# Two branch projections of a hybrid S5 and RG-LRU layer: seven products on halves in place of eight

## The chip, the cores and the metric
One core of a Trainium2 chip. The metric is the time of one execution on the device in microseconds, median of three runs; 1832.1 us before the change (1831.18 to 1832.52). Five engines work beside each other: TensorE (PE) multiplies into PSUM, VectorE (DVE), ScalarE (ACT) and GpSimd (POOL) work element by element, and SyncE (SP) issues the transfers between memory and SBUF, one behind the other in the order of its queue.

## What is computed
One layer for 512 prompt tokens and 8 x 4 sample tokens, 544 in all, in float32. After a norm, one input projection gives the inputs of two branches. Branch A (1024 channels) runs an S5 scan and a GLU, branch B (2048 channels) a convolution and a gated recurrence. The part that the change touches is the merge:

```
y = y * jax.nn.sigmoid(y @ p["s5_w_glu"] + p["s5_b_glu"])          # end of branch A, 1024 x 1024
...
y_a = y_a * jax.nn.silu(z_a)
y_b = y_b * jax.nn.silu(z_b)
merged = (jax.nn.sigmoid(g_a) * (y_a @ p["w_proj_a"])              # 1024 x 2048
          + jax.nn.sigmoid(g_b) * (y_b @ p["w_proj_b"]))           # 2048 x 2048
out = merged @ p["w_out"]                                          # 2048 x 2048
x = x + gate[:, None] * out
```

## The kernel before
Channels lie on the partitions in blocks of 128, tokens in the columns. To keep float32 accuracy, each weight and each input is split into a high and a low part (float32r): ScalarE copies the value into the high part, VectorE subtracts the high part from the value to get the low one. For 1024 weight columns a partition that is lines 144 and 145 (`split_w`), for an input block of 544 tokens lines 179 and 181 (`split_x`). One product of two blocks is then three matmuls, high x high, high x low and low x high. `product` (lines 165 to 174, matmul on line 172) does this for one block of output channels, over all blocks of input channels and both halves of the tokens (272 columns, one PSUM bank each).

Weights come by SyncE in pieces of 1 MB (`weights`, `raw`, three buffers); the high and low parts have four buffers each. Results that a later stage needs (the branch outputs `ygd` and `ybd`, the gates `zad`, `gad` and `gbd`, the gated first projection `pad`) pass through memory and come back by `loaded` into four buffers named `ld`.

The stages in question, in this order:
- GLU (lines 922 to 933): for 8 output blocks, 48 matmuls each, ScalarE takes the sigmoid, VectorE multiplies twice, and the block is split into `ah` and `al`.
- First projection (lines 936 to 948): 16 output blocks of 48 matmuls. VectorE multiplies each half with the gate from PSUM, the result goes to `pad`, and one block of the other branch's output is loaded and split into `bh`, `bl`.
- Second projection (lines 951 to 964): 16 output blocks of 96 matmuls, gated, added to what comes back from `pad`, and split for the output projection; the last eight splits follow behind the loop, when the buffers of `bh` and `bl` come free.
- Output projection (lines 974 on, matmul on line 993).

All element-wise helpers go through `tt` (line 403). The code is written in stage order; a scheduler sets the order of the instructions on each engine from its own estimate of their times, and engines keep that order. GpSimd has no work between the end of branch B and the output projection.

Of the kernel before, what the change touches and what calls it, by code (L numbers as in the profile page):

```python
# [32 lines left out]
NCH = TP // L     # chunks of the prompt  # L33
CU = 82           # columns of a group: chunks | spare | sample | sample, late
CS0 = NCH + 1     # sample sequences in the slots 0..3 (for y)
CS1 = CS0 + NS    # sample sequences in the slots 4..7 (for the last state)
WIN = 96          # columns moved in one product
CY = 74

# RG-LRU: the flat time axis, 512 prompt tokens, then 3 + 4 columns a sequence  # L40
FT = TP + NS * (TS + 3)

O_U, O_ZA, O_XB, O_ZB, O_GA, O_GB = 0, 8, 16, 32, 48, 64  # column blocks of w_in
# [12 lines left out]
def tile_hybrid_s5_rglru(  # L56
# [11 lines left out]
    dq = nc.sync      # weights  # L68
    dq2 = nc.sync   # small loads and what passes through DRAM

    const = ctx.enter_context(tc.tile_pool(name="const", bufs=1))
    wpool = ctx.enter_context(tc.tile_pool(name="wpool", bufs=4))
# [15 lines left out]
    # what passes through DRAM  # L88
# [19 lines left out]
    def exact_exp(out, x, n, e):  # L108
        """exp(x) to the last bits: 2^n times a polynomial; n and e are scratch."""
# [5 lines left out]
        # 2^n: the exponent bits of ScalarE's 2^(n + 1/4)  # L115
# [10 lines left out]
    def rsqrt_mean(eng, out, ss, u):  # L126
        """1 / sqrt(ss / D + EPS), one Newton step behind ScalarE's root; ss and u are scratch."""
# [9 lines left out]
    def split_w(src, to=None):  # L137
        """A float32 [P, 1024] as the sum of two float32r tiles."""
# [12 lines left out]
    def weights(w, col, kt, room=split_w):  # L151
        """Columns of w as stationary operands: (block, k) -> (high, low)."""
# [908 lines left out]
```

## Time and profile before

| | |
|---|---|
| median of three runs | 1832.1 us |
| profiled execution, first to last instruction | 1828.9 us |
| TensorE busy | 1755.0 us (96%), 13,420 matmuls |
| VectorE, ScalarE, GpSimd busy | 930.7 us (51%), 738.0 us (40%), 149.5 us (8%) |
| transfers | 281.58 MB, 154 GB/s on average |

The span of the profiled execution is 3.2 us shorter than the median of the timed runs, which also hold what lies around the instructions. Busy shares are averages over stages; the windows by stage in the rows below cut the span at the starts of the GLU (about 1275), of the first projection (1324), of the second (1421) and of the output projection (1616).

### The profile page before, as it was taken

The numbers are of one execution on the slowest core, as the hardware profiler recorded it, in microseconds if no ns is written. First come the engines' busy times: TensorE is split into PE (matmuls) and PEld (weight loads), VectorE is DVE, ScalarE is ACT, GpSimd is POOL, SyncE is SP. The second block draws the span as 40 slices with busy tenths as digits, with TensorE's granted clock in tenths as the row PEclk, the third lists the DMA queues.
The fourth block names the chain that finished last, engine by engine and source line by source line (L and its number), as shares of the span: only waits on it lengthen the run. The fifth ranks groups of instructions, "written<-read, shape, count | busy, mean of one in ns | idle before, by whom it ended". The sixth has DMA issues, their size and how long they took to land.

```text
span 1828.9 us, 32708 instructions
## 1 busy us (share of the span) xinstructions
PE 1755.0 (96%) x13420; PEld 1691.1 (92%) x13420; DVE 930.7 (51%) x1584; ACT 738.0 (40%) x1134; POOL 149.5 (8%) x385
## 2 busy tenths in 40 slices
PE   7879999999959999999999999999999999999997
PEld 4558999999949999999999999999999999999997
DVE  4695255547973223324556565655543433355654
ACT  7774232332212222223555545555333322234543
POOL 2100000000000000011222122321000000000000
PEclk9899999999979999999999999999999999999999
DMA  9787535444235546443444453542677644376682
GB/s 327 261 283 189 132 93 138 110 117 111 79 86 134 138 106 167 124 132 109 142 134 118 126 166 120 155 146 94 221 254 214 179 131 128 105 221 177 172 226 93
DMA packets 400280, 281.58 MB, mean 154 GB/s; under 512 B 68513, under 2 KB 350457, under 8 KB 398905
## 3 DMA queue, kind: packets, MB, share of 16 engines
q1 hardware_dynamic: 400130, 279.49, 52.5%
q8 instruction: 105, 1.72, 0.4%
q14 instruction: 45, 0.37, 0.1%
HBM read 244.64 MB, written 32.44 MB: 152 GB/s over the span
## 4 chain that ended last, share of the span: by engine, by line
PE 77%; DVE 9%; DMA 7%; ACT 3%; issue 2%; SPq 2%; POOL 0%; ACTq 0%; DVEq 0%; POOLq 0%
PE acc L172 57%; PE acc L993 11%; DVE lo L145 2%; DVE t L403 2%; DVE v L403 2%; DMA raw<-in_w_ada_dram 1%; PE pg L845 1%; PE gacc L785 1%; PE ada L218 1%; DMA raw<-in_w_in_dram 1%; DVE eh L403 1%; DMA ld<-zad 1%; PE py L652 1%; PE py L650 1%; PE pk L629 1%
## 5 line engine op out<-in xcount | busy, mean ns | idle before, releaser
L145 DVE TENSOR_TENSOR lo<-raw,hi 128x1024 fp32r<-128x1024 f32 x374 | 455.3, 1223 | 568.7 <-ACT hi L144 561.4
L172 PE MATMUL acc<-xh,hi 128*128 128x272 f32 x3424 | 719.6, 290 | 4.9 <-ACT adasb L228 2.7
L172 PE MATMUL acc<-xh,lo 128*128 128x272 f32 x3424 | 717.4, 289 | 1.3 <-DVE lo L145 1.3
L172 PE MATMUL acc<-xl,hi 128*128 128x272 f32 x3424 | 717.0, 290 | 0.2 <-DVE xl L181 0.2
L144 ACT ACTIVATE hi<-raw 128x1024 fp32r<-128x1024 f32 x374 | 391.2, 1056 | 674.9 <-PE acc L172 547.8
L172 PEld LDWEIGHTS acc<-xh,hi 128*128 128x128 f32 x3424 | 541.3, 189 | 11.0 <-ACT adasb L228 3.2
L172 PEld LDWEIGHTS acc<-xl,hi 128*128 128x128 f32 x3424 | 541.2, 189 | 1.7 <-DVE xl L181 0.5
L172 PEld LDWEIGHTS acc<-xh,lo 128*128 128x128 f32 x3424 | 539.5, 189 | 2.5 <-DVE lo L145 1.7
L993 PE MATMUL acc<-xl,hi 128*128 128x288 f32 (+1 forms) x512 | 149.3, 292 | 0.0
L993 PE MATMUL acc<-xh,hi 128*128 128x288 f32 (+1 forms) x512 | 148.6, 291 | 0.0
L993 PE MATMUL acc<-xh,lo 128*128 128x288 f32 (+1 forms) x512 | 147.3, 288 | 0.0
L993 PEld LDWEIGHTS acc<-xh,lo 128*128 128x128 f32 x512 | 96.6, 189 | 0.1
L993 PEld LDWEIGHTS acc<-xl,hi 128*128 128x128 f32 x512 | 96.5, 188 | 0.3
L993 PEld LDWEIGHTS acc<-xh,hi 128*128 128x128 f32 x512 | 96.2, 188 | 0.1
L403 DVE TENSOR_TENSOR ld<-acc,ld 128x272 f32<-128x272 f32 x64 | 25.2, 434 | 57.5 <-PE acc L172 57.5
L218 PE MATMUL ada<-lo,cs 128*72 128x512 f32 x128 | 45.3, 438 | 8.2 <-DVE lo L145 7.6
L218 PE MATMUL ada<-hi,cs 128*72 128x512 f32 x128 | 44.6, 432 | 7.4 <-ACT hi L144 7.3
L729 ACT ACTIVATE r<-pg,c 128x284 f32<-128x284 f32 x64 | 29.7, 492 | 39.7 <-PE pg L845 39.7
L650 PE MATMUL py<-eh,ca 128*128 128x96 f32 x128 | 25.7, 284 | 20.6 <-DVE eh L403 20.6
L181 DVE TENSOR_TENSOR xl<-ld,xh 128x544 fp32r<-128x544 f32 x24 | 17.3, 723 | 47.0 <-ACT xh L179 46.9
L654 ACT ACTIVATE y<-py 128x296 f32<-128x296 f32 x16 | 6.7, 419 | 85.0 <-PE py L652 66.2
L650 PEld LDWEIGHTS py<-eh,ca 128*128 128x128 f32 x128 | 20.5, 200 | 21.5 <-issue 20.8
(304 smaller groups left out, 1445.5 us busy)
## 6 DMA issues: line engine op xcount, KB each, us to landing
raw<-in_w_in_dram SPq DMA_DIRECT2D x80, 1024.0 KB
raw<-in_w_ada_dram SPq DMA_DIRECT2D x64, 512.0 KB
raw<-in_w_out_dram SPq DMA_DIRECT2D x32, 1024.0 KB
raw<-in_w_ada_dram SPq DMA_DIRECT2D x16, 1024.0 KB
raw<-in_w_proj_b_dram SPq DMA_DIRECT2D x16, 1024.0 KB
raw<-in_w_proj_a_dram SPq DMA_DIRECT2D x8, 1024.0 KB
u<-ud SPq DMA_DIRECT2D x128, 41.0 KB
gad<-sg SPq DMA_DIRECT2D x16, 272.0 KB
```

What stands on the lines that cost most here:

```text
L144: act.activation(hv, src, AF.Copy)
L145: dve.tensor_tensor(out=lv, in0=src, in1=hv, op=SUB)
L172: pe.matmul(acc[j][:, :HT], lhsT=w_, rhs=x_[k][:, j * HT:(j + 1) * HT], start=first, stop=last)
L218: pe.matmul(accs[i][:MC], lhsT=cs[:, k, :], rhs=w_[:, i * 512:(i + 1) * 512], start=first, stop=last)
L403: eng.tensor_tensor(out=out, in0=a, in1=b, op=op)
L629: pe.matmul(pk[:GC, i * P:(i + 1) * P], lhsT=bb[:, 4 * q + i], rhs=ca[:, i, 0:8].rearrange("p j c -> p (j c)"), start=True, stop=True)
L650: pe.matmul(o, lhsT=ca[:, i, 1:9].rearrange("p j c -> p (j c)"), rhs=eh[:, e0:e0 + WIN], start=True, stop=False)
L652: pe.matmul(o, lhsT=m4[:, i], rhs=u[:, c0:c0 + WIN], start=False, stop=True)
L729: turn[0] = act.activation(*args, **kw)
L785: pe.matmul(gacc[0][:MC], lhsT=cs[:, k0 + k, :], rhs=w_[:, k % 2 * 512:(k % 2 + 1) * 512], start=first, stop=last)
L845: pe.matmul(pg[:, :FH], lhsT=w_[:, g], rhs=x_[:, sl], start=first, stop=last)
L993: pe.matmul(acc[:, :t1 - t0], lhsT=w_, rhs=x_[k][:, t0:t1], start=first, stop=last)
```

## The change
Both branch projections are computed on a 2 x 2 division of the input channels (blocks 2i and 2i + 1), the output channels (two neighbouring blocks) and the tokens (two halves), by Strassen's scheme in Winograd's form: seven products of quarters, named a0, s1, s2, b0, s3, s4 and b1 after the input operand that each takes, in place of eight.
- `operand_set` makes, for two input blocks, the seven operands of 272 columns: three halves as they are, and four sums s1 to s4 in float32, on GpSimd (for the last four blocks of the second projection's input on VectorE). Each is split into high and low. The first projection takes 4 such sets, the second 8.
- `quarters` loads the weights of a group in two pieces, even and odd input blocks. `seven_head` and `seven` make the weight operands: three sums on VectorE, one (for s3) on GpSimd, and seven splits.
- A group is four output blocks in the first projection and two in the second: 7 x 24 matmuls in both. Its products accumulate in three banks; ScalarE and VectorE combine them into the output blocks (`left`, `right`).
- The gating of the first projection goes to GpSimd. The merged sums of the first 12 blocks go to memory and are loaded and split while the last group runs.
- `loaded` has three buffers in place of four, and constants that are needed only early lie in a pool of their own that is closed before the GLU, which makes room. Comments are taken out, so that line numbers move.

```diff
+    LD = 3
...
-        t = pl.tile([P, T], F32, tag="ld", name="ld", bufs=4)
+        t = pl.tile([P, T], F32, tag="ld", name="ld", bufs=LD)
...
+    def operand_set(i, sets, a, b, rooms, pl, eng=pool):
+        a0, a1, b0, b1 = a[:, :HT], a[:, HT:], b[:, :HT], b[:, HT:]
+        f = pl.tile([P, 4, HT], F32, tag="f", name="f", bufs=1)
+        s1, s2, s3, s4 = (f[:, n] for n in range(4))
+        tt(eng, s1, a1, b1, ADD)
+        tt(eng, s2, s1, a0, SUB)
+        tt(eng, s4, b0, s2, SUB)
+        tt(eng, s3, a0, a1, SUB)
+        for name, src in zip(NAMES, (a0, b0, b1, s1, s2, s3, s4)):
+            room, n = next(rooms)
+            t = room.tile([P, 2, HT], F32R, tag="xs", name="x" + name, bufs=n)
+            act.activation(t[:, 0], src, AF.Copy)
+            tt(dve, t[:, 1], src, t[:, 0], SUB)
...
+    def seven_head(w, col, kt):
+        b = quarters(w, col, kt)
+        wt = {"a0": split_q(b[0, 0])}
+        t1 = wsum(b[0, 1], b[0, 0], SUB)
+        wt["s1"] = split_q(t1)
+        return kt, b, t1, wt
...
+        t2 = wsum(b22, t1, SUB)
+        order = [("s2", lambda: t2), ("b0", lambda: b21), ("s3", lambda: wsum(b22, b12, SUB, pool)),
+                 ("s4", lambda: b22), ("b1", lambda: (tt(dve, t2, b21, t2, SUB), t2)[1])]
...
+        for name, made in order:
+            wt[name] = split_q(made())
+        acc = [[acc_tile(f"acc{x}")[:, :HT] for x in "aeb"] for _ in range(nq)]
...
+        if first:
+            run(p1, p5, p2)
+        else:
+            run(p1)
+            run(p5)
+        each(lambda a, e, b, l0, l1, r0, r1: act.activation(l0, a, AF.Copy))
+        each(lambda a, e, b, l0, l1, r0, r1: act.activation(r1, e, AF.Copy))
+        run(("s2", 0, False, True))
+        each(lambda a, e, b, l0, l1, r0, r1: act.activation(r0, a, AF.Copy))
...
+        each(lambda a, e, b, l0, l1, r0, r1: tt(dve, l0, l0, b, ADD))
+        run(("s3", 0, False, True))
+        each(lambda a, e, b, l0, l1, r0, r1: tt(dve, r1, r1, a, ADD))
+        run(("s4", 1, False, True))
+        each(lambda a, e, b, l0, l1, r0, r1: tt(dve, r0, r0, e, ADD))
+        run(("b1", 0, False, True))
+        each(lambda a, e, b, l0, l1, r0, r1: act.activation(l1, a, AF.Copy))
...
-        split_x(y_, j, ah, al)
+        if j % 2:
+            operand_set(j // 2, as_, y_last, y_, a_rooms, p3)
+        y_last = y_
...
+    head = seven_head(w_proj_a[0], 0, 8)
+    for j0 in range(0, 16, 4):
+        cs_ = seven(head, as_, j0 == 0)
+        head = seven_head(w_proj_a[0], (j0 + 4) * P, 8) if j0 < 12 else seven_head(w_proj_b[0], 0, KD)
+        for j, c in zip(range(j0, j0 + 4), cs_):
+            sg = loaded(gad, j, p3)
+            act.activation(sg, sg, AF.Sigmoid)
+            tt(pool, c, c, sg, MUL)
+            dq2.dma_start(pad[j], c)
+        for i in range(j0 // 2, j0 // 2 + 2):
+            operand_set(i, bs, loaded(ybd, 2 * i, p3), loaded(ybd, 2 * i + 1, p3), b_rooms, p3,
+                        pool if i < 6 else dve)
...
+    for j0 in range(0, 16, 2):
+        cs_ = seven(head, bs, j0 == 0)
+        if j0 < 14:
+            head = seven_head(w_proj_b[0], (j0 + 2) * P, KD)
+        else:
+            head = weights(w_out[0], 0, KD)
+            for j in range(12):
+                split_x(loaded(pad, j, p3), j, mh, ml)
+        for j, c in zip((j0, j0 + 1), cs_):
+            sg = loaded(gbd, j, p3)
+            act.activation(sg, sg, AF.Sigmoid)
+            m_ = loaded(pad, j, p3)
+            tt(dve, c, c, sg, MUL)
+            tt(dve, c, c, m_, ADD)
+            if j < 12:
+                dq2.dma_start(pad[j], c)
+            else:
+                last.append((j, c))
...
+    for j, c in last:
+        split_x(c, j, mh, ml)
```

The order of the instructions on each engine up to the GLU stage is the same as before. From there two places matter.

GpSimd before, its last rows: the end of branch B (lines 857 to 861) and then the output projection's first row.

```order
L857 MEMSET a 128x8 x2
L858 COPY r_13261<-c_318 128x8
L858 COPY r_13295<-c_318 128x8
L860 COPY stash<-r_13261 128x1
L861 COPY stash<-r_13261 128x8
L860 COPY stash<-r_13295 128x1
L861 COPY stash<-r_13295 128x8
L984 MEMSET ssq 128x15 x2
```

GpSimd now, in the first projection from the weight sum `t` of group 2 on: gatings of group 1 (`left`, `right`), operand sums of the second projection (`f`), weight sum of group 3.

```order
L405 TENSOR_TENSOR t<-raw 128x1024
L405 TENSOR_TENSOR left<-left,ld 128x544
L405 TENSOR_TENSOR right<-right,ld 128x544
L405 TENSOR_TENSOR left<-left,ld 128x544
L405 TENSOR_TENSOR f<-ld 128x272 x2
L405 TENSOR_TENSOR f<-f,ld 128x272
L405 TENSOR_TENSOR f<-ld,f 128x272
L405 TENSOR_TENSOR f<-ld 128x272 x2
L405 TENSOR_TENSOR f<-f,ld 128x272
L405 TENSOR_TENSOR f<-ld,f 128x272
L405 TENSOR_TENSOR t<-raw 128x1024
```

The weight sum of each group stands on GpSimd behind the gatings of the group two before it and the operand sums of four blocks.

VectorE before, in the first projection: one weight split, one input split and two gatings an output block, over and over.

```order
L145 TENSOR_TENSOR lo<-raw,hi 128x1024
L181 TENSOR_TENSOR xl<-ld,xh 128x544
L403 TENSOR_TENSOR ld<-acc_14244,ld 128x272
L403 TENSOR_TENSOR ld<-acc_14245,ld 128x272
L145 TENSOR_TENSOR lo<-raw,hi 128x1024
```

VectorE now, at the end of the second operand set of the second projection and the start of the third group's weights (`xb`, `xs`: low parts of operands; `right`: combination from PSUM; `lo`: low part of weights; `t`: weight sum).

```order
L405 TENSOR_TENSOR xb_14552<-ld,xb_14552 128x272
L405 TENSOR_TENSOR xb_14555<-ld,xb_14555 128x272
L405 TENSOR_TENSOR xs_14558<-f,xs_14558 128x272
L405 TENSOR_TENSOR xs_14561<-f,xs_14561 128x272
L405 TENSOR_TENSOR right<-right,acca 128x272
L405 TENSOR_TENSOR xs_14564<-f,xs_14564 128x272
L405 TENSOR_TENSOR xs_14567<-f,xs_14567 128x272
L405 TENSOR_TENSOR lo<-t,hi 128x1024
L405 TENSOR_TENSOR lo<-raw,hi 128x1024
L405 TENSOR_TENSOR t<-raw,t 128x1024
L405 TENSOR_TENSOR lo<-t,hi 128x1024
```

The first `lo` here belongs to the product s2 of group 3, and the last one reads the weight sum that GpSimd made; both stand behind all operand splits of the set, which wait for GpSimd's `f`.

## Rows read from the trace of the kernel before

**Rows 1.** The page: busy time by engine, the chain by engine and by line.

```profile
PE 1755.0 (96%) x13420; PEld 1691.1 (92%) x13420; DVE 930.7 (51%) x1584; ACT 738.0 (40%) x1134; POOL 149.5 (8%) x385
...
PE 77%; DVE 9%; DMA 7%; ACT 3%; issue 2%; SPq 2%; POOL 0%; ACTq 0%; DVEq 0%; POOLq 0%
...
PE acc L172 57%; PE acc L993 11%; DVE lo L145 2%; DVE t L403 2%; DVE v L403 2%; DMA raw<-in_w_ada_dram 1%; PE pg L845 1%; PE gacc L785 1%; PE ada L218 1%; DMA raw<-in_w_in_dram 1%; DVE eh L403 1%; DMA ld<-zad 1%; PE py L652 1%; PE py L650 1%; PE pk L629 1%
```

**Rows 2.** Windows: GLU, first projection, second; busy time (instructions), clock, transfers.

```profile
core 0: us, PE busy (x) PEld busy (x) DVE busy (x) ACT busy (x) POOL busy (x), PEclk, DMA share, GB/s
1275.00:1324.00 49.00, 48.70 (x386) 48.08 (x385) 29.64 (x40) 18.81 (x33) 6.56 (x4) 1.00 0.69 221
1324.00:1421.00 97.00, 94.81 (x737) 94.59 (x738) 38.53 (x59) 34.96 (x53) 0.00 (x0) 0.98 0.73 229
1421.00:1616.00 195.00, 195.00 (x1542) 195.00 (x1541) 74.79 (x101) 55.44 (x66) 0.00 (x0) 1.00 0.46 130
```

**Rows 3.** The chain in order of time: start, us, what; both projections.

```profile
1378.38 237.09 PE acc L172 x1872
1615.47 10.62 PE acc L993 x80
```

**Rows 4.** VectorE's groups, 1275 to 1616: busy, mean ns; idle before, releasers.

```profile
L145 DVE TENSOR_TENSOR lo<-raw,hi 128x1024 fp32r<-128x1024 f32 x57 | 69.4, 1220 | 80.8 <-ACT hi L144 80.7
L403 DVE TENSOR_TENSOR ld<-acc,ld 128x272 f32<-128x272 f32 x64 | 25.2, 434 | 57.5 <-PE acc L172 57.5
...
L403 DVE TENSOR_TENSOR ld<-ld,sg 128x544 f32<-128x544 f32 x8 | 5.8, 720 | 0.1
```

**Rows 5.** Timeline of VectorE and GpSimd, 939 to 950: start, us, what.

```profile
943.27 6.02 POOL L860 COPY stash<-r 128x1 f32<-128x1 f32 x1 [2.66 <-DVE r L859]
...
949.36 0.18 POOL L860 COPY stash<-r 128x1 f32<-128x1 f32 x1
...
941.88 2.55 DVE L859 TENSOR_TENSOR_SCAN r<-a,r 128x568 f32<-128x568 f32 x2
944.37 2.32 DVE L145 TENSOR_TENSOR lo<-raw,hi 128x1024 fp32r<-128x1024 f32 x2
946.62 1.48 DVE L403 TENSOR_TENSOR zb<-zb,r 128x512 f32<-128x512 f32 x4
948.03 1.21 DVE L145 TENSOR_TENSOR lo<-raw,hi 128x1024 fp32r<-128x1024 f32 x1
949.16 0.17 DVE L236 TENSOR_TENSOR a<-pt,a 128x36 f32<-128x36 f32 x1
```

**Rows 6.** Timeline of VectorE, 984 to 987.

```profile
985.18 0.42 DVE L403 TENSOR_TENSOR wgl<-wg,wgh 128x256 fp32r<-128x256 f32 x1
985.52 0.74 DVE L403 TENSOR_TENSOR r<-r,cv 128x568 f32<-128x568 f32 x1
```

**Rows 7.** ScalarE's groups, 1275 to 1616.

```profile
L144 ACT ACTIVATE hi<-raw 128x1024 fp32r<-128x1024 f32 x57 | 59.8, 1053 | 97.0 <-PE acc L172 96.9
...
L940 ACT ACTIVATE ld<-ld 128x544 f32<-128x544 f32 x16 | 10.5, 658 | 46.8 <-DMA ld<-gad 35.7 <-issue 10.8
...
L929 ACT ACTIVATE sg<-acc,c 128x272 f32<-128x272 f32 x16 | 6.8, 474 | 0.0
```

**Rows 8.** Timeline of GpSimd, a copy and an addition of 512.

```profile
563.99 1.09 POOL L664 COPY g__5728<-yc 128x512 f32<-128x512 f32 x1 [1.39 <-DMA yc<-yd]
...
803.43 1.57 POOL L403 TENSOR_TENSOR fin<-spre,eh 128x512 f32<-128x512 f32 x1
```

**Rows 9.** Timeline of VectorE and GpSimd, 790 to 793.

```profile
790.76 1.65 DVE L145 TENSOR_TENSOR lo<-raw,hi 128x1024 fp32r<-128x1024 f32 x1 [5.53 <-ACT hi L144]
...
790.22 1.11 POOL L664 COPY g__7990<-yc 128x512 f32<-128x512 f32 x1 [1.98 <-DMA yc<-yd]
```

**Rows 10.** The chain in the GLU stage: loads of a gate block, issue to landing.

```profile
1295.57 2.51 DMA ld<-zad
...
1302.84 4.27 DMA ld<-zad
```

More of the change, by code (lines that the diff above doesn't have):

```diff
@@ L917, in tile_hybrid_s5_rglru, with split_q, wsum @@
     st2.close()
+    ste.close()
     st3, p3 = phase("p3")
-    ah, al = [None] * 8, [None] * 8
+    ROOM[id(p3)] = 8
+    def split_q(src):
+        hi, lo = (wpool.tile([P, 1024], F32R, tag=t, name=t) for t in ("hi", "lo"))
+        hv, lv = (v.rearrange("p (q i m) -> p q i m", q=src.shape[1], m=P) for v in (hi, lo))
+        act.activation(hv, src, AF.Copy)
+        tt(dve, lv, src, hv, SUB)
+        return hi, lo
+    def wsum(x, y, op, eng=dve):
+        t = p3.tile([P, 1024], F32, tag="t", name="t", bufs=2)
+        v = t.rearrange("p (q i m) -> p q i m", q=x.shape[1], m=P)
+        tt(eng, v, x, y, op)
+        return v
@@ new lines, in quarters @@
+    def quarters(w, col, kt):
+        n, nq = kt // 2, 16 // kt
+        out = {}
+        for s in range(2):
+            raw = raw_tile()
+            dq.dma_start(raw.rearrange("p (i m) -> p i m", i=n),
+                         w[:, col:col + nq * 256].rearrange("(i s p) m -> s p i m", s=2, p=P)[s])
+            v = raw.rearrange("p (i q h m) -> p h q i m", i=n, q=nq, h=2)
+            for h in range(2):
+                out[s, h] = v[:, h]
+        return out
+    def seven_head(w, col, kt):
[4 more added lines that the diff above has]
+        return kt, b, t1, wt
@@ new lines, in seven, with run, each @@
+    def seven(head, sets, first=False):
+        kt, b, t1, wt = head
+        n, nq = kt // 2, 16 // kt
+        b12, b21, b22 = b[0, 1], b[1, 0], b[1, 1]
+        t2 = wsum(b22, t1, SUB)
+        order = [("s2", lambda: t2), ("b0", lambda: b21), ("s3", lambda: wsum(b22, b12, SUB, pool)),
+                 ("s4", lambda: b22), ("b1", lambda: (tt(dve, t2, b21, t2, SUB), t2)[1])]
+        if first:
+            order[0], order[1] = order[1], order[0]
+        for name, made in order:
+            wt[name] = split_q(made())
+        acc = [[acc_tile(f"acc{x}")[:, :HT] for x in "aeb"] for _ in range(nq)]
+        left = [wk.tile([P, T], F32, tag="z", name="left", bufs=2) for _ in range(nq)]
+        right = [wk.tile([P, T], F32, tag="sg", name="right", bufs=2) for _ in range(nq)]
+        def run(*products):
+            for i in range(n):
+                for name, bank, new, done in products:
+                    for q in range(nq):
+                        h, l = (v[:, (q * n + i) * P:(q * n + i + 1) * P] for v in wt[name])
+                        xh_, xl_ = sets[name][i]
+                        for w_, x_, f, e in ((h, xh_, i == 0, False), (h, xl_, False, False),
+                                             (l, xh_, False, i == n - 1)):
+                            pe.matmul(acc[q][bank], lhsT=w_, rhs=x_, start=new and f, stop=done and e,
+                                      skip_group_check=True)
+        def each(f):
+            for q in range(nq):
+                f(*acc[q], left[q][:, :HT], left[q][:, HT:], right[q][:, :HT], right[q][:, HT:])
+        p1, p5, p2 = ("a0", 0, True, True), ("s1", 1, True, True), ("b0", 2, True, True)
+        if first:
+            run(p1, p5, p2)
[6 more added lines that the diff above has]
+        each(lambda a, e, b, l0, l1, r0, r1: act.activation(r0, a, AF.Copy))
+        if not first:
+            run(p2)
+        each(lambda a, e, b, l0, l1, r0, r1: tt(dve, l0, l0, b, ADD))
[5 more added lines that the diff above has]
+        each(lambda a, e, b, l0, l1, r0, r1: act.activation(l1, a, AF.Copy))
+        return [v for q in range(nq) for v in (left[q], right[q])]
@@ L922, in tile_hybrid_s5_rglru @@
+    as_ = {}
+    a_rooms = in_rooms((xpool, 28))
     for j in range(8):
@@ new lines, in tile_hybrid_s5_rglru @@
+    mh, ml = [None] * KD, [None] * KD
+    last = []
+    for j0 in range(0, 16, 2):
[16 more added lines that the diff above has]
+                last.append((j, c))
+        if j0 < 5 * 2:
+            rows_out(j0 // 2 * P)
@@ L986, in tile_hybrid_s5_rglru @@
         for j in range(KD):
-            wts = weights(w_out[0], j * P, KD)
+            wts = head if t0 and j == 0 else weights(w_out[0], j * P, KD)
             acc = acc_tile("acc")
```

46 lines of the change are left out of this document (13 added, 33 removed).

## The prediction, made before the changed kernel ran

> **What bounds the kernel now.** I read the page's shares and chain first: TensorE is busy 96% of the span, and 77% of the chain that ended last is TensorE, 57% on the one matmul line of all projections [rows 1]. The windows by stage then show where it waits: in the GLU stage and in the second projection it is busy all the time, in the first projection 94.8 of 97 us (some records are missing), at a granted clock of 0.98 to 1.00 [rows 2]. VectorE is busy 60% of the GLU stage and about 39% of both projections, ScalarE less, GpSimd not at all in the projections [rows 2]. So here a matmul removed is time gained, until another engine's work per matmul grows past it. The chain gives the price of one: 1872 matmuls in 237.09 us, 0.1266 us each, with no gap at the step to the output projection [rows 3].
>
> **Matmuls.** Before, the two projections are 16 x 48 + 16 x 96 = 2304 matmuls of 272 columns. After, each group (four output blocks of the first, two of the second) is 7 products x 24 = 168, and there are 4 + 8 groups: 2016. Gain: 288 x 0.1266 = 36.5 us. A group is 168 x 0.1266 = 21.3 us of TensorE; that is the time in which every other engine must do its share of it.
>
> **VectorE, ScalarE and GpSimd per group.** A VectorE subtraction of 128x1024 is 1.22 us [rows 4], 1.125 us from start to start in a run of them (2.25 us for two) [rows 5]. One of 128x544 is 0.72 [rows 4], some 0.65 in a run. One of 128x272 from SBUF isn't in the trace; between the 128x256 one (0.34 us to the next start) [rows 6] and half of the 544, I take 0.35. From PSUM the 128x272 is 0.43 [rows 4].
> In the first projection a group has 7 low parts and 3 weight sums of 1024 (11.2 us), 14 low parts of the operands of the second projection (4.9) and 6 combinations from PSUM (2.6): 18.7 us. ScalarE has 7 high parts at 1.05, 8 copies from PSUM at 0.47, 4 sigmoids at 0.66 and 14 high parts of 272 from SBUF, taken at 0.43, a tenth under the copy from PSUM: 19.8 us [rows 7]. Both fit into 21.3, barely.
> GpSimd gets one weight sum of 1024, four gatings of 544 and eight operand sums of 272, 5376 elements. Its only float32 addition of size in the trace took 1.57 us for 512, 3.06 ns an element; a copy of 512 took 1.09, 2.13 ns [rows 8]. So 16.5 us, at least 11.4. Taken alone this fits too.
>
> **What speaks against it: the two engines don't work side by side.** A VectorE subtraction that started while GpSimd copied took 1.65 us in place of 1.22, ending 1.2 us after the copy [rows 9]. A GpSimd copy of one element a partition, 0.18 us elsewhere, took 6.02 us: it came back at 949.29, when VectorE's unbroken run of instructions with two SBUF inputs ended at 949.24 and one that reads PSUM began [rows 5]. So the terms add: 16.1 us of VectorE from SBUF and 16.5 of GpSimd are 32.6 us a group (27.5 at the copy's rate), against 21.3 of TensorE.
> The Trainium skill ("SBUF — State Buffer", "Who interferes with whom") has this as a lock that VectorE instructions with two SBUF inputs and GpSimd instructions that read SBUF hold for one whole instruction each; the trace agrees on the exclusion, but its 6.02 us are several instructions, so a waiting GpSimd can be passed over. With a wait of one instruction the engines would alternate, which is my forecast; with passing over it is rival C.
>
> **How much of it lands on TensorE.** In the order of the changed program the weight splits of group 3 stand on VectorE behind all operand splits of blocks 0 to 3, those wait for GpSimd's sums, and these stand behind the gatings of group 1 on GpSimd's queue (order blocks in the section on the change). Nothing can be put off, so the sum counts. From the last split of group 2 to the last split of the first group of the second projection VectorE has 56 us from SBUF (three times 16.1, and the last time 14 operand splits and 8 sums of 272 more, 7.8) and GpSimd 15,584 elements, 47.7 us (33.2 at least): 104 us (89), where TensorE has three groups, 64 us. The four buffers of split weights let VectorE be three products ahead, 9 us. That leaves 31 us (16). Handing over between engines, and input loads that VectorE and GpSimd wait for (2.5 to 4.3 us from issue to landing in the GLU stage [rows 10], now with three buffers of them in place of four), I put at a tenth of the 104, 10 us; from 0, if all of it hides, to 20. Slip: 41 us, bounds 16 to 60.
>
> **The two ends of the change.** Start: blocks 6 and 7 of the GLU's output now pass through four GpSimd sums, 3.3 us, and seven splits. TensorE has 54 matmuls of the first group (6.8 us) that don't need them: 2 us, bounds 0 to 8. The loads of the GLU stage now also wait until a set's sums release the two buffers they read; at 12.2 us of TensorE for two blocks this just fits. End: twelve blocks of the merged sum come back from memory and are split next to seven weight splits, some 12 x 0.65 + 7 x 1.125 + gating and splits of the last four 5 = 21 us of VectorE, while TensorE has the last product (3 us) and the first two or three output blocks (6.4 us each by 10.62 us for 80 matmuls [rows 3]): 5 us, bounds 0 to 12.
> Second projection, groups 2 to 8: VectorE from SBUF 10 x 1.125 + 4 x 0.65 = 13.9, from PSUM 1.3, GpSimd one sum of 1024, 3.1: 18.3 of 21.3 us. TensorE stays the bound; nothing.
> All before the GLU stage has the same order of instructions on every engine: nothing. The weight loads have the same bytes in longer runs, in front of TensorE as before: nothing. Waits may also lower TensorE's granted clock (0.98 in the first projection before [rows 2]); while VectorE and GpSimd are the bound this costs nothing more, and I add no term.
>
> **Sum.** -36.5 + 41 + 2 + 5 = +11.5 us on the profiled span of 1828.9, 1840.4; the median lies 3.2 us above that span (1832.1), which is outside the instructions and stays: 1843.6.
>
> **Rivals.**
> A is the forecast, 1844: faster work on TensorE, paid back in the first projection because GpSimd and VectorE exclude each other. Chance 0.43.
> B: the exclusion costs TensorE nothing, since GpSimd runs in the gaps in which VectorE waits for ScalarE's high parts (VectorE waits 80.7 us for them in this stretch [rows 4]) and both stay under 21.3 us a group. Then only the ends count: 1832.1 - 36.5 + 7 = 1802.6. For it: VectorE is far from full before. Against it: after the change it has 18.7 of 21.3 us of its own. Chance 0.22.
> C, still slower: GpSimd is passed over for as long as VectorE has work, as in the 6.02 us of [rows 5], in the second projection too. It decides once VectorE's gaps in a group fall below the 3.1 us of the weight sum that the fourth product needs; 21.3 - 15.2 = 6.1 us of gaps are there, but in pieces. A loss of 3 us in each of seven groups on top of A gives 1865. Chance 0.20.
> D, no change: the additions cost what the copy does, and the slip is its lower bound of 16 + 10 us: 1843.6 - 15 = 1828.6. Chance 0.15.
> The Trainium skill ("GPSIMD Engine Reference", "Elementwise — side-by-side cycle accounting") gives 4497 ns for a float32 addition of 2048, by which an estimate of one element is 2.2 ns, close to the copy's rate in [rows 8] and below the row of the addition; by it the time would be D's.
>
> **Chances and range.** No change is within 0.2%, 3.7 us, of 1832.1 (what a measurement here can tell). Faster: all of B, half of D, and little of A, 0.32. Same: a third of D and some of A, 0.12. Slower: most of A and all of C, 0.56. A's own range, from its slip of 31 to 60 us, is 1833 to 1863. The range to hold 8 in 10 must reach B on one side, since leaving B out would leave out more than 2 in 10, and past C on the other: 1802 to 1872.
>
> **What would show it.** Right: 288 matmuls fewer; in the first projection TensorE is busy some two thirds of a stage that is longer than the 97 us of before, its idle time ended by VectorE's low parts or ScalarE's high parts of weight sums, and these by GpSimd; VectorE subtractions of 1024 well above 1.22 us and GpSimd additions of 544 well above 1.7 while the other works; the second projection at 21.3 us a group with TensorE full. For B: a first projection of about 85 us. For C: TensorE waits in each group of the second projection before the product with the GpSimd sum. For D: GpSimd additions of 1024 near 2.2 us where nothing runs beside them. The forecast is wrong if the first projection is shorter than before, or if the long waits stand at the ends, where I have 7 us.

## The result, and the profile after

The changed kernel takes 1845.2 us (median of five runs, 1835.9 to 1846.1) against 1832.1 us before: a ratio of 1.0064, 95% interval 1.0039 to 1.0089. The forecast was 1843.6 us; slower by more than 0.2% had the chance 0.56. The profiled execution is the fastest of the five (1835.9 us). It reached the last gate matmul ahead of the GLU 5.9 us earlier than the profiled execution of the kernel before, by the same instructions. So the stages are read here from that matmul on, a point that both kernels share. Its row of before and of after (tile `gacc`: shortest, median, longest, first and last start):

```profile
L785 PE MATMUL gacc<-hi,cs x64: 390/392/393, 863.7 to 1269.1; 128*72 128x512 f32 x64
```
```profile
L810 PE MATMUL gacc<-hi,cs x64: 390/392/393, 857.9 to 1263.2; 128*72 128x512 f32 x64
```

Before, 559.8 us follow that point (span 1828.9), after, 570.9 (span 1834.1): 11.1 us more, what the ratio gives too (0.64% of 1832 are 11.7). With 36.5 us of matmuls saved, 47.6 us were paid back. (Each span is that of one execution.)

The page of the changed kernel, busy time and chain by engine, as in [rows 1]:

```profile
PE 1728.5 (94%) x13132; PEld 1658.4 (90%) x13132; DVE 1093.0 (60%) x1724; ACT 806.3 (44%) x1294; POOL 253.7 (14%) x453
...
PE 68%; DVE 11%; DMA 10%; ACT 4%; issue 3%; POOL 3%; SPq 2%; ACTq 0%; DVEq 0%; POOLq 0%
```

There are 288 matmuls fewer, and TensorE's share of the chain fell by nine points, which went mostly to VectorE, transfers and GpSimd. The windows by stage, which answer to [rows 2]: first projection, first group of the second, its other seven groups, output projection; then a piece of the second row. (A group begins at its first matmul; neighbours can overlap by a product.)

```profile
core 0: us, PE busy (x) PEld busy (x) DVE busy (x) ACT busy (x) POOL busy (x), PEclk, DMA share, GB/s
1312.40:1421.90 109.50, 88.92 (x632) 85.31 (x631) 102.91 (x113) 63.15 (x125) 65.11 (x43) 0.94 0.56 175
1421.90:1460.00 38.10, 27.04 (x171) 24.14 (x169) 32.90 (x49) 19.89 (x41) 13.51 (x9) 0.82 0.61 185
1460.00:1612.30 152.30, 151.41 (x1201) 150.73 (x1202) 122.49 (x122) 68.54 (x95) 16.89 (x9) 1.00 0.58 176
1612.30:1834.10 221.80, 206.51 (x1642) 204.09 (x1640) 126.55 (x223) 105.58 (x167) 0.00 (x0) 0.98 0.68 196
...
1444.00:1460.00 16.00, 13.31 (x67) 11.08 (x67) 14.20 (x29) 10.37 (x22) 0.03 (x1) 0.69 0.58 171
```

What a stretch lost is its length less 0.1266 us for each matmul of the projections in it. (The counts in the rows also hold a few transposes and matmuls that reach over an edge.) The first projection's stretch, 109.5 us, holds 625 of its 672 matmuls, 79.1 us: 30.4 lost. The other 47 stand behind the second projection's first matmul. The next stretch, 38.1 us, holds 168 matmuls of both, 21.3 us: 16.8 lost. The other seven groups, 152.3 us, hold 1199, 151.8 us: 0.5 lost. The output projection's stretch, 221.8 us, holds the last 24 (3.0 us) beside the 213.4 us that it took before (from the start in [rows 3] to the end of the span): 5.4 lost. That is 53.1 us.

The kernel before lost some 5 us of its own in the first projection. Counted by matmuls, its GLU (384) began at 1269.6, its first projection (768) ran from 1318.3 to 1420.8, and not from 1324, where the windows of [rows 2] are cut. That is 102.4 us for 97.2 us of matmuls, at a clock of 0.98 and with this wait:

```profile
1327.80 0.52 PE L172 MATMUL acc<-xh,hi 128*128 128x272 f32 x2 [2.19 <-ACT xh L179]
```

With the 53.1 us less these 5.2, the 47.6 us are accounted for to 0.3.

Two things stand out. The first is VectorE and GpSimd. VectorE's groups in the first projection (1312.4 to 1421.9), a subtraction with both inputs in SBUF and one that reads PSUM:

```profile
L405 DVE TENSOR_TENSOR lo<-t,hi 128x1024 fp32r<-128x1024 f32 x15 | 23.4, 1566 | 1.4 <-ACT hi L952 1.4
...
L405 DVE TENSOR_TENSOR right<-right,acca 128x272 f32<-128x272 f32 x6 | 2.6, 432 | 3.3 <-PE acca L1008 3.3
```

The first took 1220 ns before [rows 4], the second is where it was (434). The timelines of VectorE and of GpSimd at one place (start, us, what):

```profile
1399.51 1.22 DVE L405 TENSOR_TENSOR lo<-t,hi 128x1024 fp32r<-128x1024 f32 x1
1400.65 4.52 DVE L405 TENSOR_TENSOR xs<-f,xs 128x272 fp32r<-128x272 f32 x3
1405.09 2.39 DVE L405 TENSOR_TENSOR lo<-t,hi 128x1024 fp32r<-128x1024 f32 x1
1407.40 1.59 DVE L405 TENSOR_TENSOR xs<-f,xs 128x272 fp32r<-128x272 f32 x1
1408.91 1.21 DVE L405 TENSOR_TENSOR t<-raw,t 128x1024 f32<-128x1024 f32 x1
...
1400.81 2.53 POOL L405 TENSOR_TENSOR t<-raw 128x1024 f32<-128x1024 f32 x1 [3.10 <-DVE lo L405]
1403.30 1.56 POOL L405 TENSOR_TENSOR right<-right,ld 128x544 f32<-128x544 f32 x1
1404.83 3.86 POOL L405 TENSOR_TENSOR left<-left,ld 128x544 f32<-128x544 f32 x2
```

Three subtractions of 272, some 1.1 us elsewhere in this kernel, took 4.52 us while GpSimd added 1024 elements and gated 544: singly 0.43, 2.64 and 1.60 us, the second ending 0.3 us after GpSimd's sum and the third 0.3 us after its gating. The 1024 behind them took 2.39 beside the next gatings, and a sum of 1024 took 1.21 once GpSimd was done.

The second is input loads. The chain that ended last at the start of the second projection, in order of time (start, us, what):

```profile
1419.26 7.01 DMA ld<-ybd
...
1426.43 2.65 POOL f L405 x3
...
1429.16 1.66 POOL f L405
1430.83 2.48 DMA ld<-gad
1433.31 2.33 POOL left L405
1435.64 1.56 POOL right L405
...
1437.58 5.65 DMA ld<-ybd
...
1445.96 2.99 DMA ld<-ybd
...
1452.12 3.82 PE acca L1008 x22
1455.94 2.75 PE acce L1008 x22
```

A load can start only when GpSimd or VectorE frees one of three buffers, GpSimd goes on when it has landed, and so in turn; four loads of this chain are 18.1 us. At the third of these loads, ScalarE's timeline and TensorE's next matmul:

```profile
1441.96 0.66 ACT L1061 ACTIVATE ld<-ld 128x544 f32<-128x544 f32 x1 [6.41 <-DMA ld<-gad]
1443.25 0.43 ACT L786 ACTIVATE xa<-ld 128x272 fp32r<-128x272 f32 x1 [0.63 <-DMA ld<-ybd]
```
```profile
1443.74 0.60 PE L1008 MATMUL acca<-xa,hi 128*128 128x272 f32 x1 [5.57 <-ACT xa L786]
```

ScalarE waits 6.41 us for a gate, and the operand copy that TensorE needs stands behind that wait. But the copy then waits another 0.63 us for its own load, so here it is the load that holds TensorE, and the order on ScalarE costs nothing. Behind TensorE's gap of 5.57 us the granted clock is 0.69 (1444 to 1460, above), part of the time at 1.2 and part at 2.4 GHz: the 22 matmuls from 1452.12 take 0.174 us each, the next 22 0.125.

### The profile page after: what moved, and what is told of

Its sections match the earlier page's. It is cut to its first block, busy times and chain, and to the rows that moved or that the text cites. A ratio compares the mean times of both kernels' runs of the same rounds, so it can differ in the third digit from the quotient of the medians.

```text
span 1834.1 us, 32739 instructions
## 1 busy us (share of the span) xinstructions
PE 1728.5 (94%) x13132; PEld 1658.4 (90%) x13132; DVE 1093.0 (60%) x1724; ACT 806.3 (44%) x1294; POOL 253.7 (14%) x453
## 4 chain that ended last, share of the span: by engine, by line
PE 68%; DVE 11%; DMA 10%; ACT 4%; issue 3%; POOL 3%; SPq 2%; ACTq 0%; DVEq 0%; POOLq 0%
PE acc L174 42%; PE acc L1120 9%; PE acca L1008 4%; PE acce L1008 2%; DVE lo L147 2%; DVE t L405 2%; DVE v L405 2%; DMA ld<-pad 2%; PE ada L220 1%; PE pg L870 1%; PE gacc L810 1%; DMA raw<-in_w_in_dram 1%; DMA ld<-ybd 1%; SPq L642 1%; POOL f L405 1%
## 5 line engine op out<-in xcount | busy, mean ns | idle before, releaser
L174 PE MATMUL acc<-xh,hi 128*128 128x272 f32 x2656 | 558.5, 290 | 2.8 <-ACT adasb L230 2.8
L174 PE MATMUL acc<-xh,lo 128*128 128x272 f32 x2656 | 557.7, 289 | 1.3 <-DVE lo L147 1.3
L174 PE MATMUL acc<-xl,hi 128*128 128x272 f32 x2656 | 555.3, 289 | 0.0
L174 PEld LDWEIGHTS acc<-xh,hi 128*128 128x128 f32 x2656 | 419.9, 189 | 8.5 <-ACT adasb L230 3.3
L174 PEld LDWEIGHTS acc<-xh,lo 128*128 128x128 f32 x2656 | 418.2, 188 | 2.5 <-DVE lo L147 1.7
L174 PEld LDWEIGHTS acc<-xl,hi 128*128 128x128 f32 x2656 | 418.9, 189 | 1.0 <-issue 0.2
L1120 PEld LDWEIGHTS acc<-xh,hi 128*128 128x128 f32 x512 | 96.0, 188 | 3.2 <-ACT xh L181 2.9
L1120 PEld LDWEIGHTS acc<-xh,lo 128*128 128x128 f32 x512 | 96.4, 188 | 1.0 <-DVE lo L147 0.9
L1120 PEld LDWEIGHTS acc<-xl,hi 128*128 128x128 f32 x512 | 96.3, 189 | 0.5 <-DVE xl L183 0.3
L1008 PE MATMUL acce<-xs,hi 128*128 128x272 f32 x384 | 78.8, 297 | 6.3 <-ACT right L1022 3.3
L405 DVE TENSOR_TENSOR lo<-t,hi 128x1024 fp32r<-128x1024 f32 x48 | 70.6, 1473 | 14.9 <-ACT hi L952 14.5
L1008 PE MATMUL acca<-xs,hi 128*128 128x272 f32 x384 | 75.7, 294 | 0.4 <-ACT right L1024 0.4
L1008 PEld LDWEIGHTS acce<-xs,hi 128*128 128x128 f32 x384 | 62.7, 194 | 8.3 <-ACT right L1022 4.0
```

Source lines behind the costliest of these rows:

```text
L174: pe.matmul(acc[j][:, :HT], lhsT=w_, rhs=x_[k][:, j * HT:(j + 1) * HT], start=first, stop=last)
L405: eng.tensor_tensor(out=out, in0=a, in1=b, op=op)
L1008: pe.matmul(acc[q][bank], lhsT=w_, rhs=x_, start=new and f, stop=done and e, skip_group_check=True)
L1120: pe.matmul(acc[:, :t1 - t0], lhsT=w_, rhs=x_[k][:, t0:t1], start=first, stop=last)
```

## The experiments

Each edit is made in the changed kernel. Ratios are to the kernel before, run on the same chip beside it; "under the changed kernel" is the difference of the two ratios times 1832 us. The theories: VectorE and GpSimd exclude each other (1), input loads through three buffers (2), GpSimd as a mere slow link (3).

**Nothing on GpSimd in the first projection.**

```diff
-            tt(pool, c, c, sg, MUL)
+            tt(dve, c, c, sg, MUL)
...
-                        pool if i < 6 else dve)
+                        dve)
...
-("s3", lambda: wsum(b22, b12, SUB, pool)),
+("s3", lambda: wsum(b22, b12, SUB, dve if kt == 8 else pool)),
```

> In the first projection GpSimd gets nothing: gatings, operand sums of the second projection and the weight sum of the third product go to VectorE, everything else as in the changed kernel. Theory 1 (VectorE and GpSimd exclude each other, and the sum of both sets the pace of the first projection): VectorE then has 56 us from SBUF, 8 from PSUM and 3 x 6.5 for what it takes over, 83 us without a competitor, against 64 us of three groups on TensorE and a lead of 9; with 8 us of hand-overs a slip of some 18 us in place of 41: 1822 us, between 1815 and 1830, with VectorE subtractions of 1024 back at 1.2 us. Theory 2 (input loads through three buffers set the pace): no change, 1841 to 1849. Theory 3 (GpSimd is only a slow link in a chain, VectorE isn't held up by it): also some 1822.

Measured: 1832.15 us against 1827.56, ratio 1.0018 (1.0004 to 1.0032), 8 us under the changed kernel where 23 were expected by theories 1 and 3, and none by theory 2. VectorE's subtractions are back at 1219 ns, but with GpSimd's work added VectorE is busy 94.1 of the stage's 102.4 us (windows in the next experiment). The longest wait of TensorE in the stage, in group 3, shows on ScalarE:

```profile
1382.65 0.66 ACT L1061 ACTIVATE ld<-ld 128x544 f32<-128x544 f32 x1 [5.13 <-DMA ld<-gad]
1383.47 0.40 ACT L1022 ACTIVATE right<-acce 128x272 f32<-128x272 f32 x1 [0.16 <-DMA pad<-right]
```
and in the waits of 1360 to 1390 (in total, times, longest):
```profile
PE acce L1008 <- ACT right L1022: 7.3, 1, 7.3
```

TensorE waits 7.3 us for a PSUM bank, which the second line's copy frees. The copy stands behind the sigmoid of a gate that lands late, but what ended its own wait, 0.16 us after the sigmoid, is the store of the result that it writes over. VectorE's gating of that result and the issue of its store:

```profile
1378.86 0.72 DVE L405 TENSOR_TENSOR right<-right,ld 128x544 f32<-128x544 f32 x1
```
```profile
1379.60 0.32 SPq L1063 DMA_DIRECT2D pad<-right  x1
```

So a third limit shows here: a group's results must be gated and stored before the next group's copies can have their tiles. By these rows an earlier gate load alone would not have shortened the gap.

**The same, with additions on GpSimd whose results nobody uses.**

```diff
+    d_ = p3.tile([P, 2, P], BF16, name="idle")
+    two = ident[:, None, :].to_broadcast([P, 2, P])
...
             tt(dve, c, c, sg, MUL)
+            tt(pool, d_[:, 0, :2], c[:, :2], c[:, :2], ADD)
+            for _ in range(5):
+                tt(pool, d_, two, two, ADD)      # 128x256, from a constant
```

> As the run with everything on VectorE, but GpSimd does 20 additions of 128x256 a group (five behind each gating, about 0.8 us each, 16 us a group) that read a constant and that nobody waits for. Theory 1: the additions cost VectorE as much time as the useful ones did, so the time goes back to 1840 us or above (up to 1870, since VectorE now has more of its own), with VectorE subtractions of 1024 at 1.5 us or more. Theory 3 (slow link only) and theory 2 (loads): the same as the run without them, within 3 us.

Measured: 1852.49 us, ratio 1.0129 (1.0106 to 1.0152), 20.3 us more than without them. The first projection by windows without and with the additions, and in the second kernel VectorE's two kinds of subtraction, GpSimd's additions (busy, mean ns) and two waits of ScalarE (in total, times, longest):

```profile
1313.20:1415.60 102.40, 88.50 (x654) 86.34 (x654) 94.14 (x147) 61.50 (x125) 8.07 (x8) 0.93 0.63 194
```
```profile
1316.70:1438.10 121.40, 93.10 (x655) 87.93 (x654) 117.40 (x155) 65.49 (x132) 71.00 (x80) 0.93 0.54 167
...
L405 DVE TENSOR_TENSOR lo<-t,hi 128x1024 fp32r<-128x1024 f32 x15 | 19.9, 1329 | 0.0
L405 DVE TENSOR_TENSOR right<-right,acca 128x272 f32<-128x272 f32 x7 | 3.0, 426 | 0.2 <-PE acca L1008 0.2
...
L405 POOL TENSOR_TENSOR idle<-ident 128x256 bf16<-128x256 f32 x60 | 52.3, 872 | 4.7
...
ACT left L1021 <- POOL idle L405: 6.5, 2, 3.7
ACT right L1022 <- POOL idle L405: 5.6, 2, 4.6
```

Nobody uses the additions' results, and yet VectorE's subtractions from SBUF are longer, 1329 ns in place of 1219, while those that read PSUM are not (426): VectorE is held up by GpSimd as such, where theory 3 expected nothing. (1.5 us or more were expected of the 1024.) The price isn't one for one: set against their undisturbed lengths (0.43, 0.72 and 1.22 us), VectorE's instructions in the stage took 23.7 us more with the additions and 3.6 without, so 62.9 us more of GpSimd cost VectorE 20.1 us. (The rest of the 23.3 us by which its busy time grew are eight instructions more in the longer stretch.)

The time isn't the price of this alone. The small addition that places the five others behind a gating reads the gated tile, and ScalarE's copies for the next group write over that tile. They waited 12.1 us for it in four places (last two lines), and three waits of TensorE, of 2.1, 2.9 and 5.2 us, end with such a copy. How much of the 19.0 us of the stage is VectorE's delay and how much this, the run doesn't part.

**Six input buffers.**

```diff
-    LD = 3
+    LD = 6
...
+            if i == 7 and name in ("b1", "s3", "s4"):
+                sets[name][i] = sets["a0"][i]
+                continue
```

> Six input buffers in place of three. The room for them is gained by leaving out three of the seven operand splits of the last block pair of the second projection, which uses the first operand there; some 2 us less of ScalarE and VectorE. Theory 1: the loads explain only the waits that the trace names a load for, some 5 to 6 us in front of the second projection: 1838 to 1843 us. Theory 2: the chain from a freed buffer over a load of 3 to 4 us to the next gating sets the pace; six buffers take most of the 41 us of slip away: 1815 to 1830 us.

Measured: 1829.49 us against 1827.56, ratio 1.0002 (0.9988 to 1.0016), 11 us under the changed kernel. Neither expectation: more than theory 1 allowed, less than theory 2 wanted. The windows of the first projection and of the group behind it tell where:

```profile
1317.10:1428.50 111.40, 90.62 (x632) 87.94 (x631) 102.46 (x112) 65.99 (x133) 68.38 (x46) 0.89 0.56 177
```
```profile
1428.50:1458.10 29.60, 24.57 (x167) 23.52 (x166) 27.06 (x39) 14.81 (x27) 11.38 (x5) 0.88 0.63 192
```

The first projection isn't shorter (111.4 against 109.5), where VectorE and GpSimd still work beside each other; the group behind it is, 29.6 us in place of 38.1. So most of the gain lies at another place, where the loads stood. Not all of it need be the loads': the edit also leaves out three operand splits there, some 2 us of ScalarE and VectorE by the expectation.

**Both edits together.**

> Both edits together: nothing on GpSimd in the first projection and six input buffers (three of the operand splits of the last pair left out for their room). If there are two limits, one behind the other, the gains add or more than add: the run on VectorE alone stood 8 us under the changed kernel and still had a 7.3 us gap of TensorE behind a gate load and some 9 us of late loads at the start of the second projection; 8 + 7 + 11 = 26 us under the changed kernel, 14 us under the kernel before, between 8 and 20 under it. If both edits remove the same wait, the better of the two alone stays: 11 us under the changed kernel, level with the kernel before (within 3 us).

Measured: 1820.56 us against 1830.78, ratio 0.9956 (0.9938 to 0.9973), 20 us under the changed kernel: the sum of both (8.4 + 11.4), each of them known to some 5 us. From the common point on, the profiled executions give 15.7 us, where the two edits alone give 7.9 and 11.3 (table below). So most of both gains stays, and neither limit hides the other; whether they add in full isn't shown. The 26 us in the expectation counted the 7.3 us gap on top of the 11.

**GpSimd's part left out.**

```diff
-            tt(pool, c, c, sg, MUL)
...
+        if sets is bs and i < 6:
+            s1, s2, s3, s4 = a1, b1, a0, b0
...
-("s3", lambda: wsum(b22, b12, SUB, pool)),
+("s3", lambda: b22 if kt == 8 else wsum(b22, b12, SUB, pool)),
```

> The changed kernel with GpSimd's part of the first projection left out and given to nobody: no gating there (the gates are loaded and their sigmoid taken, but not multiplied in), no operand sums for blocks 0 to 11 of the second projection (their splits read the input halves), no weight sum for the third product (its quarter is split as it is). Loads, stores, ScalarE and VectorE's own instructions are as in the changed kernel; a gate's buffer comes free at its sigmoid in place of its gating. If GpSimd's work costs the first projection through VectorE, VectorE's subtractions of 1024 are back at 1.22 us, its busy time in the first projection falls from 102.9 us to some 75, and the first projection from 109.5 us to between 85 and 93: 15 to 25 us under the changed kernel, 4 to 13 us under the kernel before. If its cost is only that of the moved work (8 us, as in the run on VectorE alone) and the loads hold the rest, 6 to 10 us under the changed kernel.

Measured: 1814.49 us against 1831.58, ratio 0.9915 (0.9892 to 0.9938), 27 us under the changed kernel. The windows of the first projection and of the group behind it, and VectorE's subtraction in the first:

```profile
1319.80:1418.20 98.40, 88.81 (x656) 86.35 (x655) 80.16 (x124) 64.92 (x137) 8.22 (x8) 0.95 0.64 202
1418.20:1442.30 24.10, 21.23 (x147) 19.68 (x145) 20.74 (x35) 14.34 (x29) 2.41 (x1) 0.93 0.74 226
...
L405 DVE TENSOR_TENSOR lo<-t,hi 128x1024 fp32r<-128x1024 f32 x12 | 14.7, 1221 | 4.2 <-ACT hi L955 2.8 <-PE accb L1011 1.4
```

More than the 15 to 25 us expected. VectorE's time in the first projection fell by 22.7 us (102.9 to 80.2), the stage itself by 11 only, to 98.4 and not to 93 (with 24 matmuls, 3 us, more in it), and the group behind it fell by 14: its operands now come without GpSimd's sums between two loads, and buffers come free earlier. The run can't part these two, so 27 us is what GpSimd's part costs with what it does to the loads.

**One projection alone by seven products.** The second alone (the first as before the change, its operand sums on VectorE), and the first alone (the second as before):

> Seven products for the second projection alone; the first is done by eight as before the change, and VectorE makes the operand sums of the second beside it, GpSimd is silent there. Theory 1: the second projection keeps its gain of 8 x 24 matmuls of 0.1266 us, 24.3 us, and VectorE with 15.6 us for each 24.3 us of TensorE holds nobody up; 5 us at the step to the output projection and 3 us of late operands at its start stay: 1832 - 24 + 8 = 1816 us, between 1810 and 1822. Rival (the loss lies in the scheme itself, in the start of the second projection and in its end, not in what the first projection's helpers cost): 1832 us or more.

> Seven products in the first projection alone; the second is done by eight as before the change, so its operands are plain splits of 544 and the operand sums are gone. GpSimd keeps the gatings and the third product's weight sum. From the changed kernel's own rows a group has 13.9 us of VectorE from SBUF, 2.1 from PSUM and some 8 of GpSimd: 22 us with exclusion against 21.3 on TensorE, so nearly no slip from it; the 12 us of 96 matmuls saved are left less 8 to 14 us of hand-overs, gate loads and the start: between 4 us under and 4 us over the kernel before. If instead the seven-product scheme of the first projection costs by itself what it costs in the changed kernel (changed kernel less the run with the second projection alone, 15 us), it is 10 to 15 us over the kernel before.

Measured: the second alone 1825.58 us against 1827.56, ratio 0.9981 (0.9967 to 0.9996), 3.5 us under the kernel before where 16 were expected. The first group of seven products took 28.9 us and the second 24.2, and ScalarE stood 4.8 and 8.2 us before gate loads at their start: the loads again, although GpSimd was silent. Here the order on ScalarE does cost TensorE time. A copy of weights stands behind the second of these waits, starts without a wait of its own, and ends a wait of TensorE:

```profile
1417.81 0.66 ACT L1056 ACTIVATE ld<-ld 128x544 f32<-128x544 f32 x1 [8.24 <-DMA ld<-gad]
1418.37 1.04 ACT L952 ACTIVATE hi<-raw 128x1024 fp32r<-128x1024 f32 x1
```
```profile
1419.46 0.52 PE L1008 MATMUL accb<-xb,hi 128*128 128x272 f32 x2 [3.70 <-ACT hi L952]
```

The first alone: 1836.61 us against 1831.28, ratio 1.0031 (1.0014 to 1.0048), 5.7 us over: between the two expectations. Its subtractions of 1024 from weight sums took 1432 ns in the mean, so the gatings and the weight sum on GpSimd are enough to stretch them.

**Four input buffers with nothing left out.** In the changed kernel (v_ld4), in the one with everything on VectorE (v_dve4, v_dve4b) and in the one with the second projection alone (v_second4, v_second4b). Room came from writing s3 and s4 over input halves, in the two kernels with a b from writing s4 over s1 and taking the tile of the state rows from `ld`:

```diff
-        f = pl.tile([P, 4, HT], F32, tag="f", name="f", bufs=1)
+        f = pl.tile([P, 2, HT], F32, tag="f", name="f", bufs=1)     # v_...4: s3, s4 = a1, b0
+        f = pl.tile([P, 3, HT], F32, tag="f", name="f", bufs=1)     # v_...4b: s4 = s1
```

> Four input buffers in place of three, nothing left out: the operand sums s3 and s4 are written over input halves that are no longer needed, which makes the room. GpSimd works as in the changed kernel. If the wait is for a free buffer behind a load of 3 to 4 us, one more buffer takes half or more of what six took: 5 to 11 us under the changed kernel. If it needs all four gate loads of a group beside two operand loads, less than 3 us.

> Nothing on GpSimd in the first projection and four input buffers, nothing left out. With two limits: 8 us for VectorE alone and most of 7 + 11 us for the buffers: 14 to 24 us under the changed kernel, 2 to 12 us under the kernel before. With one shared limit: level with the kernel before.

> Seven products in the second projection alone, sums on VectorE, four input buffers, nothing left out. With three buffers this stood 3.5 us under the kernel before; ScalarE stood 8.2 and 4.8 us in front of gate loads, TensorE 3.7 and 3.0 us behind it at the start of the second projection. If the loads are the cause these gaps and the low clock behind them go: some 8 us more, 8 to 15 us under the kernel before. If the start of the second projection is late because of operand splits themselves, 3 to 5 us under it, as with three.

> Seven products in the second projection alone, sums on VectorE, four input buffers as in v_second4, but the room comes from other places (a sum written over one that is already split; the small tile of the state rows taken from the input buffers), so no input half is kept longer than with three. If v_second4 lost its gain because its buffers were held until the last sum was split, this is 10 to 14 us under the kernel before; if four buffers don't help here, 4 to 7 us, as the two before.

> Nothing on GpSimd in the first projection and four input buffers gained in the same way, nothing left out. v_dve4 stood 10 us over the run with three buffers, with a wait of ScalarE of 14 us for a gate load whose buffer an input half written over by a sum still held. If that holding was the cause, this is level with or under the run with three buffers: between 4 us over and 8 us under the kernel before. If four buffers as such bring another order that is worse, 10 us over again.

| | ratio to the kernel before | us to it |
|---|---|---|
| v_ld4 | 1.0038 (1.0024 to 1.0052) | +7 |
| v_dve4 | 1.0073 (1.0059 to 1.0086) | +13 |
| v_second4 | 0.9964 (0.9947 to 0.9981) | -7 |
| v_second4b | 1.0000 (0.9984 to 1.0016) | 0 |
| v_dve4b | 0.9969 (0.9950 to 0.9987) | -6 |

v_dve4 went wrong at one place. ScalarE's timeline, and the queue of SyncE at the same time:

```profile
1436.93 0.42 ACT L787 ACTIVATE xs<-ld 128x272 fp32r<-128x272 f32 x1
1451.69 0.66 ACT L1062 ACTIVATE ld<-ld 128x544 f32<-128x544 f32 x1 [14.34 <-DMA ld<-gad]
```
```profile
SPq L969 <- POOL t L405: 10.6, 1, 10.6
```

The gate load stood on SyncE's queue behind a weight load that waited 10.6 us for GpSimd's weight sum to free its buffer. In v_dve4b the wait for that sum is 1.9 us, and it is 19 us faster. v_second4b, meant as the better of its pair, isn't. So four buffers don't decide by themselves; at the one place looked at, the order of loads on the queue did. v_dve4b, v_second4 and the second projection alone leave nothing out and are faster than both kernels.

The runs stood on several chips. As a check, the time from the last gate matmul to the end, in each run's one profiled execution:

| | us | to before | to changed |
|---|---|---|---|
| before | 559.8 | | |
| changed | 570.9 | +11.1 | |
| all on VectorE | 563.0 | +3.2 | -7.9 |
| the same with additions | 583.2 | +23.4 | +12.3 |
| six buffers | 559.6 | -0.2 | -11.3 |
| both edits | 555.2 | -4.6 | -15.7 |
| GpSimd's part left out | 546.4 | -13.4 | -24.5 |
| second alone | 557.4 | -2.4 | -13.5 |
| first alone | 563.9 | +4.1 | -7.0 |
| v_ld4 | 565.6 | +5.8 | -5.3 |
| v_dve4 | 575.8 | +16.0 | +4.9 |
| v_second4 | 557.0 | -2.8 | -13.9 |
| v_second4b | 558.1 | -1.7 | -12.8 |
| v_dve4b | 553.4 | -6.4 | -17.5 |

Against the kernel before they agree with the ratios to 4 us. v_second4 and v_second4b are 1.1 us apart here, so the 7 us between their ratios aren't shown to come from the edit.

## Why the prediction was right

**The sum.** Matmuls: 288 fewer, as forecast. Start: 2 us forecast, 4.4 measured (waits of 1.6 and 2.8 us behind the GLU's last sigmoids, inside the first projection's 30.4). Slip: 41 us forecast; 30.4 + 16.8 less the start's 4.4 are 42.8 against full rate, and 37.6 more than in the kernel before, which lost 5.2 there itself. End: 5 us forecast, 5.4 measured. Second projection from its second group: nothing forecast, 0.5 measured. 37.6 + 4.4 + 5.4 + 0.5 are 47.9 us, where 48 were forecast. The time came out 1.6 us from the forecast, and that is partly luck: terms inside the slip were off and cancelled, as told below.

Two readings of the prediction don't hold. It put the 2.2 us in which TensorE stood idle in the first projection [rows 2] down to missing records; they were a wait, all 768 matmuls are on record, and the kernel before was 5 us off full rate there. (And the 1.2 us behind the copy in [rows 9] are 1.08.) Its upper bound of 60 us for the slip has no working: 31 + 20 are 51. Of its signs, TensorE busy for two thirds of the first projection did not come: it was busy 88.9 of 109.5 us.

**The mechanism.** Exclusion was the main term. That GpSimd holds VectorE up is shown: 1329 ns in place of 1219 beside additions whose results nobody uses. What it costs in time is only bounded: 27 us came back without GpSimd's part, but that frees buffers too, and 20 us came with the additions, but those also held up ScalarE's copies. The three subtractions of 0.43, 2.64 and 1.60 us beside GpSimd's 2.53 and 1.56 fit a wait of one whole instruction at a time, not GpSimd passed over for long. The Trainium skill ("SBUF — State Buffer", "Who interferes with whom") says that a VectorE instruction with two SBUF inputs contends with a GpSimd instruction that reads SBUF, and one with at most one SBUF input doesn't; the 1566 ns and 432 ns above agree. That section of the Trainium skill words the hold for a whole instruction, which the prediction takes from it, for VectorE's two-port modes; for these subtractions it is the timeline above that shows it.

**What was mis-sized inside the sum.** Three terms were off and cancelled each other. GpSimd's price: 3.06 ns an element came from an addition of 512 [rows 8]; with little beside it, the sums of 1024 in the second projection (1465 to 1612) took

```profile
L405 POOL TENSOR_TENSOR t<-raw 128x1024 f32<-128x1024 f32 x7 | 16.7, 2391 | 133.5 <-DVE lo L405 133.5
```

2.33 ns an element, near rival D's premise. The Trainium skill ("GPSIMD Engine Reference", "Elementwise — side-by-side cycle accounting") gives 4497 ns for 2048, an estimate of 2.2 ns an element; the measured row lies nearer to it than to [rows 8]. Second, the two engines' times don't add in full: 62.9 us of GpSimd cost VectorE 20.1. Third, against these, the loads and hand-overs: 10 us forecast, "a tenth of the 104", where six buffers (and three splits less) gave 11 us back and a buffer chain made most of the second projection's late start. So 31 us of exclusion and 17 us of the rest were forecast; taking GpSimd's part away gave 27 back and left 21, though that edit frees buffers too.

The profile before held a sign of the loads [rows 7]: ScalarE's sigmoids of gates waited 35.7 us for them there, while TensorE stayed nearly full. In the changed kernel no wait of TensorE is shown to come from such a sigmoid; with the second projection alone one of 3.7 us stands behind one. The forecast took ScalarE's 19.8 us a group as work that fits, and not its order, nor the order of loads and stores behind it.

**Clock.** No term was forecast. In the late start of the second projection it is one: 16 us at 0.69 are up to 5 us, within the 16.8. In the first projection no run here parts it from the waits.

**The rivals.** B (exclusion costs nothing, a first projection of 85 us) is out: 109.5. Even without GpSimd's part it is 98.4. C (GpSimd passed over, waits in every group) is out: seven groups at TensorE's rate. D had nearly the right price of a GpSimd addition and the wrong time, 1828.6; that the loads made up the difference is argued from the runs with more buffers, not shown by one run.

## What to carry to other kernels

Saving TensorE work pays only as far as the helpers' time per group fits, and here GpSimd wasn't a free fourth helper beside a VectorE that subtracts from SBUF: giving VectorE the work gained 8 us, with more buffers some 17 (v_dve4b). Giving GpSimd only what runs while VectorE reads PSUM or waits was not tried. An engine's wait for a load in the old profile is worth a look once urgent work is put behind it on the same engine: count buffers against loads per group, and look at what stands on the transfer queue in front of the load, and at which wait ended last, the load's or the store's. Where two limits lie at different places, test them alone and together; here most of both gains remained.

## What was not expected of the hardware

GpSimd's hold on VectorE was partial: 0.32 us of VectorE for each us of GpSimd's additions (20.1 of 62.9). What it cost a single instruction went with GpSimd's instruction and not with VectorE's own length: beside a gating of 544 a subtraction of 1024 went from 1.22 to 2.39 us and one of 272 from 0.43 to 1.59, and beside a GpSimd sum of 1024 one of 272 took 2.64.
